# Conditioning products moved from GpSimd to TensorE in a fused 2+2-layer transformer kernel

## The chip, the cores and the metric

The kernel runs as one program on one core of one Trainium2 chip. The metric is the time of the program on the device in microseconds, as the median of several runs. Beside the runs there is one profiled execution, from which all rows come; it has a time of its own.

## The reference, cut to what matters

Two blocks of two layers follow one another on 256 tokens of width 1024, all in fp32. The second block is conditioned on one vector `c`: each of its two layers takes six rows of 1024 values (shift, scale and gate for the mixer and for the feed-forward part) from one product.

```python
x = first_block(x, mem, positions, ...)      # layer 0: pooled/latent attention; layer 1: gated recurrence
                                             # each: + cross attention to mem, + SwiGLU
cond = jax.nn.silu(c)                        # second block
for i in range(2):
    mod = cond @ ada_w[i] + ada_b[i]         # (1024) @ (1024, 6144): six rows
    sh_m, sc_m, g_m, sh_f, sc_f, g_f = split(mod, 6)
    h = rms_norm(x, norm_mix[i]) * (1 + sc_m) + sh_m
    y = dsa_attention(h) if i == 0 else s5_mixer(h)
    x = x + g_m * y
    h = rms_norm(x, norm_ffn[i]) * (1 + sc_f) + sh_f
    x = x + g_f * conv_ffn(h)
```

There are thus 12 rows of `mod`; each needs a 1024x1024 block of `ada_w`, which is 8 chunks of 128x1024 fp32 (512 KB), 96 chunks in all.

## The kernel before, in words

**Weights.** Nearly all products run on TensorE (PE) with each fp32 weight split in two fp32r parts. A chunk of 128x1024 is loaded by the queue of SyncE (SP) into a `raw` buffer; ScalarE (ACT) writes `hi` as a rounded copy (line 319); VectorE (DVE) writes `lo = raw - hi` (line 320; a few on POOL). PE then makes three products per operand pair (line 403, `mm`). Three `raw` and four `hi`/`lo` buffers exist, more in stages that open a ring (`ring`): `r1` (two more raw, three more split) holds from the first cross attention to the end of the first feed-forward part, `r4` (two more raw) in the sparse attention.

**Order.** `Builder` collects a list of steps in program order; each engine runs its own instructions in that order. Inside a stage the order is a string of two-letter codes: `EORD` (latent attention, `even`), `XORD` (cross attention, `xattn`), `OORD` (recurrence, `odd`), `DORD` (sparse attention, `dsa`). Work off to the side goes in two ways: a list `fill`, drawn by `gap`, and "lanes" (`side`), generators of which `add` puts a piece behind a step for every so many weight chunks that steps have used.

**Stages,** in us of the profile: latent attention 0 to 136, cross attention to 228, SwiGLU (`ffn(0)`) to 441, recurrence to 580, second cross attention to 650, second SwiGLU (`ffn(1)`) to 895, sparse attention (`dsa`) to 1070, convolutional feed-forward (`ffn(2)`) to 1293, state-space mixer to 1383, `ffn(3)` to the end. Between two stages `head` turns the normalised rows `h` by PE transposes (line 525, `norm_b`) into `xh`, `xl`.

**The conditioning rows** are made by `ada_gen` in a lane. SP loads a chunk into `fr` (line 733). POOL multiplies it by the column of silu(c) for its 128 inputs (line 752; line 750 for a row's first chunk) and adds it to `acc` (line 753). After eight chunks PE sums `acc` over the partitions with a 128x32 matrix of ones: four products, one for each 256 columns, each with its 32 output partitions (`w<-acc,ones`). DVE adds the bias (line 768), and a scale row is also multiplied by its norm's gain (line 770). Rows 0 to 7 are made from 50 us to the end of the recurrence, rows 10, 8, 9 in `ffn(2)`, row 11 in `ffn(3)`. `resid` and `mod_rows` use them later from DRAM.

**Attention values.** `pair_pv` multiplies the values of two heads by their probabilities. The values lie in `VP`, each head padded with 64 columns of zeros, so that the four products (two heads, two blocks of keys) all write 128 partitions of one bank. POOL fills `VP` with zeros first (lines 870, 1514).

**Second memory.** The cross attention of layer 1 has its own norm of `mem`. In `XORD` the steps `a0` to `a3` load it (from ACT's queue), take its squares (`na`), scale it (`na2`, line 683) and turn it (`nb`); `a2` and `a3` stand at the end.

**Tables.** `dsa_tables` and `odd_tables` (rotation tables and constants of the recurrence: some 50 DVE instructions on small tiles) are each one step of `ffn(0)`, behind its groups 6 and 12 of 22.

## Time and profile before

| | |
|---|---|
| median of 3 runs | 1596.26 us (1594.91 to 1597.49) |
| the profiled execution's own time | 1588.07 us |
| its span, first to last instruction | 1586.3 us |
| PE busy | 1437.9 us (91%) |
| DVE, ACT, POOL busy | 1227.6, 772.9, 719.5 us |
| mean granted clock of TensorE | 0.961 of full speed |
| chain that ended last | PE 37%, DVE 18%, ACT 6%, issue 4%, DMA 3%, POOL 1% of the span |
| read from memory | 302.45 MB, 198 GB/s over the span |

A busy share is an average over ten stages with different limits. Idle time of PE counts where the list of waits names what ended it. The granted clock stands at one of two levels, 2.4 GHz (1.0) and 1.2 GHz (0.5); in a window that mixes both, the mean stands between.

### The profile page before, as it was taken

Reading aid. Unit: us, or ns where it says so; the run is one execution under the profiler, and the core shown is the slowest. Engines: PE = TensorE matmul, PEld = TensorE weight load, DVE = VectorE, ACT = ScalarE, POOL = GpSimd, SP = SyncE. Lnnn points to the kernel's source line nnn. Section 1 sums busy time; section 2 is a strip of 40 time slices with the busy share of each in tenths; the row PEclk is TensorE's granted clock in tenths of the full one; section 3 lists DMA queues with packets and bytes.
Section 4 is the critical chain, followed back from the end, with each engine's and each line's share of the span. In section 5 each row is a group of like instructions: output and inputs, shape, how many; then the busy total and the mean of one; then the engine's idle time right before and its main releaser. Section 6 shows DMA issues by size and latency. Waiting matters only on the chain.

```text
span 1586.3 us, 25647 instructions
## 1 busy us (share of the span) xinstructions
PE 1437.9 (91%) x9852; PEld 1286.4 (81%) x9852; DVE 1227.6 (77%) x1734; ACT 772.9 (49%) x1286; POOL 719.5 (45%) x570
## 2 busy tenths in 40 slices
PE   8898989989998999899879698998999957899998
PEld 8787979978897879799778576678889845799997
DVE  5766577978957876877999779556887967689865
ACT  5654445334444765544434353656455543465542
POOL 4764567797965311412577522111864524105100
PEclk9999999999999999999989998999999979999999
DMA  6546758685754554665565444325887755667650
GB/s 239 201 175 236 257 178 275 233 319 215 282 184 152 161 184 148 211 220 168 208 202 169 161 137 142 107 67 187 299 281 279 266 123 178 221 229 255 220 177 27
DMA packets 90315, 316.24 MB, mean 199 GB/s; under 512 B 10464, under 2 KB 15504, under 8 KB 88912
## 3 DMA queue, kind: packets, MB, share of 16 engines
q1 hardware_dynamic: 77760, 277.57, 51.3%
q0 software_dynamic: 7216, 27.59, 5.3%
q10 hardware_dynamic: 5216, 9.44, 1.7%
q8 instruction: 77, 1.26, 0.3%
q14 instruction: 46, 0.38, 0.1%
HBM read 302.45 MB, written 11.06 MB: 198 GB/s over the span
## 4 chain that ended last, share of the span: by engine, by line
PE 37%; DVE 18%; ACT 6%; issue 4%; DMA 3%; POOL 1%; ACTq 0%; DVEq 0%; POOLq 0%
PE w L403 20%; PE a L403 13%; DVE lo L320 7%; ACT hi L319 2%; DMA raw<-in_down 2%; PE gl L403 1%; DVE sv L1935 1%; DVE cy L1267 1%; DMA raw<-in_up 1%; DMA U<-h 1%; DVE cy L1273 0%; DVE x L533 0%; PE w L525 0%; DVE h L480 0%; ACT e L813 0%
## 5 line engine op out<-in xcount | busy, mean ns | idle before, releaser
L320 DVE TENSOR_TENSOR lo<-raw,hi 128x1024 fp32r<-128x1024 f32 (+2 forms) x420 | 625.1, 1516 | 110.8 <-ACT hi L319 109.8
L319 ACT ACTIVATE hi<-raw 128x1024 fp32r<-128x1024 f32 (+2 forms) x430 | 437.5, 1047 | 111.0 <-DMA raw<-in_up 28.7
L403 PE MATMUL w<-xh,hi 128*128 128x256 f32 x1696 | 474.6, 285 | 16.0 <-DVE sg L1248 14.8
L403 PE MATMUL w<-xh,lo 128*128 128x256 f32 x1696 | 476.9, 285 | 10.3 <-DVE lo L320 9.7
L403 PE MATMUL w<-xl,hi 128*128 128x256 f32 x1696 | 466.4, 284 | 0.0
L403 PEld LDWEIGHTS w<-xh,hi 128*128 128x128 f32 x1696 | 322.5, 192 | 24.2 <-DVE sg L1248 15.7
L403 PEld LDWEIGHTS w<-xh,lo 128*128 128x128 f32 x1696 | 323.1, 192 | 14.2 <-DVE lo L320 14.2
L403 PEld LDWEIGHTS w<-xl,hi 128*128 128x128 f32 x1696 | 318.8, 191 | 3.1 <-ACT hi L319 0.2
L753 POOL TENSOR_TENSOR acc<-acc,fr 128x1024 f32<-128x1024 f32 x84 | 222.7, 2651 | 7.0
L752 POOL TENSOR_SCALAR fr<-fr,cs 128x1024 f32<-128x1024 f32 x84 | 168.4, 2005 | 126.2 <-DMA fr<-in_ada 125.5
L403 PE MATMUL a<-hi,gl 128*128 128x512 f32 x352 | 114.0, 398 | 7.2 <-DVE gl L397 7.2
L403 PE MATMUL a<-hi,gh 128*128 128x512 f32 x352 | 115.3, 401 | 4.0 <-ACT hi L319 3.2
L403 PE MATMUL a<-lo,gh 128*128 128x512 f32 x352 | 114.2, 398 | 0.6 <-DVE lo L320 0.5
L1267 DVE SCALAR_TENSOR_TENSOR cy<-w,cols,cy 128x254 f32<-128x254 f32 (+1 forms) x176 | 72.5, 473 | 23.9 <-ACT cy L1263 23.9
L403 PEld LDWEIGHTS a<-hi,gl 128*128 128x128 f32 x352 | 67.1, 191 | 23.0 <-DVE gl L397 7.8
L1247 ACT ACTIVATE sg<-w 128x256 f32<-128x256 f32 x44 | 16.8, 382 | 133.2 <-PE w L403 133.2
L403 PEld LDWEIGHTS a<-lo,gh 128*128 128x128 f32 x352 | 66.9, 190 | 17.2 <-DVE lo L320 2.0
L403 PEld LDWEIGHTS a<-hi,gh 128*128 128x128 f32 x352 | 61.7, 191 | 15.5 <-ACT hi L319 4.0
L396 ACT ACTIVATE gh<-cy 128x256 fp32r<-128x256 f32 x44 | 18.4, 418 | 95.0 <-DVE cy L1273 95.0
L500 POOL TENSOR_SCALAR sp<-ss 128x1 f32<-128x1 f32 x18 | 6.2, 345 | 121.9 <-ACT h L487 100.7
L750 POOL TENSOR_SCALAR acc<-fr,cs 128x1024 f32<-128x1024 f32 x12 | 16.5, 1376 | 93.0 <-DMA fr<-in_ada 51.1
L1263 ACT ACTIVATE cy<-w,cols 128x256 f32<-128x256 f32 x88 | 44.6, 557 | 28.2 <-PE w L403 27.8
(446 smaller groups left out, 2588.4 us busy)
## 6 DMA issues: line engine op xcount, KB each, us to landing
raw<-in_up SPq DMA_DIRECT2D x176, 512.0 KB, 4.4
fr<-in_ada SPq DMA_DIRECT2D x96, 512.0 KB, 5.2
raw<-in_down SPq DMA_DIRECT2D x88, 512.0 KB, 4.5
raw<-in_xa_k SPq DMA_DIRECT2D x16, 512.0 KB, 4.4
raw<-in_xa_v SPq DMA_DIRECT2D x16, 512.0 KB, 4.3
raw<-in_xa_q SPq DMA_DIRECT2D x16, 512.0 KB, 5.2
raw<-in_xa_o SPq DMA_DIRECT2D x16, 512.0 KB, 4.9
raw<-in_od_in SPq DMA_DIRECT2D x16, 512.0 KB, 3.3
```

Of the source, the lines that this page charges most:

```text
L319: nc.scalar.activation(hi[:, :n], t[:, :n], AF.Copy)
L320: (nc.gpsimd if j in self.lo_pool else nc.vector).tensor_sub(lo[:, :n], t[:, :n], hi[:, :n])
L396: nc.scalar.activation(hi, src, AF.Copy)
L403: self.nc.tensor.matmul(out, lhsT=a, rhs=b, start=start, stop=stop)
L500: g.tensor_scalar(p, ss[0], 1.0 / D, EPS, op0=OP.mult, op1=OP.add)
L750: g.tensor_scalar(acc, w, c, 0.0, op0=OP.mult, op1=OP.add)
L752: g.tensor_scalar(w, w, c, 0.0, op0=OP.mult, op1=OP.add)
L753: g.tensor_add(acc, acc, w)
L1247: nc.scalar.activation(sg, p[:, 0:S], AF.Silu)
L1263: nc.scalar.activation(y, u, AF.Identity, bias=cb[:, f:f + 1], scale=cw[:, 3 * f + 2:3 * f + 3])
L1267: nc.vector.scalar_tensor_tensor(y[:, s:], u[:, :S - s], cw[:, 3 * f + 2 - s:3 * f + 3 - s], y[:, s:], op0=OP.mult, op1=OP.add)
L1935: lambda e=e, out=out, p=p: e.tensor_mul(out, *p), lambda e=e, t=t, q=q: e.tensor_mul(t, *q),
```

## The change

**Products on PE.** `ada_gen` and its lanes go; so do the matrix of ones and all of POOL's multiplications and additions for the rows. Now `ada_mm(n)` takes n loaded chunks and makes four products for each on PE, with silu(c)'s column, repeated 32 times, as the stationary operand and 256 columns of the chunk as the moving one, all n accumulated in one bank. DVE then adds the bank to the row `modr`, which starts as the bias (line 777 of the changed kernel). SP loads the next chunks behind it. The places are written out: `i2` in the order strings is a pair of chunks, `ada=(2, 2, 0)` puts a pair ahead of each transposition of a head, and `ffn(2)` takes one chunk behind each of its groups 2 to 15. In all there are 41 pairs and 14 single chunks: 8 pairs in the latent attention, 4 in the cross attention, 2 in `ffn(0)`, 6 in the recurrence, 16 in `dsa`, 14 singles and a pair in and behind `ffn(2)`, 4 pairs in `ffn(3)`. Rows 5 to 8 are now made in `dsa`, where none was made, 10 and 9 in `ffn(2)`. The chunks have 4 buffers up to the recurrence, 3 in `dsa`, 2 after it.

**Values not padded.** `VP` holds the values alone, without zeros and without the fill. Each product of `pair_pv` has 64 stationary columns and writes its head's 64 partitions.

**Second memory.** `a0` to `a3` stand earlier and further apart in `XORD`; the load is issued by POOL.

**Tables.** `dsa_tables` and `odd_tables` become generators in a lane, a piece of one to three instructions for each chunk that `ffn(0)` uses.

**Smaller.** `r4` gives one more raw buffer in place of two. The order strings change elsewhere by the `i2` alone, and by `A0` ahead of `u3` in `EORD`.

```diff
-XORD = ('q0 q2 q4 f0 s0 s1 q6 p0 s2 p1 r0 a0 s3 w0 r1 p2 w1 r2 w2 p3 w3 a1 r3 w4 w5 a2 a3', 'q0 =0 q2 s0 q4 s1 p0 s2 q6 p1 r0 s3 r1 =1 p2 w0 w1 p3 w2 r2 w3 r3 w4 w5')
+XORD = ('q0 q2 q4 f0 s0 a0 s1 q6 p0 s2 i2 p1 r0 s3 a1 w0 r1 p2 i2 a2 w1 r2 w2 p3 i2 w3 r3 a3 w4 w5', 'q0 =0 q2 s0 q4 s1 p0 s2 q6 p1 r0 s3 r1 =1 p2 w0 w1 p3 w2 r2 w3 r3 w4 w5')
...
-OORD = 'x0 x1 g0 e0 x2 x3 f1 g1 e1 f1 R0 b0 g2 g3 l0 e2 s1 e3 f1 b1 f1 R1 s0 o0 f1 b2 f6 s2 b3 s3 d0 d1 o1 f1 f1 d2 d3 d4 d5'
...
+OORD = 'x0 x1 i2 g0 e0 x2 x3 f1 g1 e1 f1 i2 R0 b0 g2 g3 l0 e2 s1 e3 f1 i2 b1 f1 R1 s0 o0 f1 i2 b2 f6 s2 b3 s3 d0 d1 o1 f1 f1 d2 d3 d4 d5'
...
-    def head(self, fills=(0, 0, 0)):
+    def head(self, fills=(0, 0, 0), ada=(0, 0, 0)):
...
         for t in range(2):
             self.gap(fills[t])
+            self.ada_fill(ada[t])
             self.add((lambda t: lambda w: self.norm_b(t))(t))
         self.gap(fills[2])
+        self.ada_fill(ada[2])
...
-    def sincos(self, pool, ang, out_c, out_s, shape, tag):
+    def sincos_steps(self, pool, ang, out_c, out_s, shape, tag):
...
             nc.vector.tensor_scalar(n, ang, INV2PI, turn, op0=OP.mult, op1=OP.add)
+            yield
             nc.vector.tensor_scalar(n, n, MAGIC, None, op0=OP.add)
             nc.vector.tensor_scalar(n, n, -MAGIC, None, op0=OP.add)
             nc.vector.scalar_tensor_tensor(r, n, -PI_A, ang, op0=OP.mult, op1=OP.add)
+            yield
...
-    def ada_gen(self, rows, late=False):
-
-        nc, g = self.nc, self.nc.gpsimd
...
-            for k in range(8):
-                load()
-                w, c = tiles.pop(0), self.cs[:, k:k + 1]
-                if k == 0:
-                    g.tensor_scalar(acc, w, c, 0.0, op0=OP.mult, op1=OP.add)
-                else:
-                    g.tensor_scalar(w, w, c, 0.0, op0=OP.mult, op1=OP.add)
-                    g.tensor_add(acc, acc, w)
...
-            p = self.ps()
-            for j in range(4):
-                self.mm(p[32 * j:32 * j + 32, 0:256], self.ones, acc[:, 256 * j:256 * j + 256], True, True)
...
+            self.ada_rows = list(rows)
+            self.ada_todo = [8 * r + k for r in rows for k in range(8)]
...
+        self.steps.append((f, ()))
+
+    def ada_load(self):
+        while self.ada_todo and len(self.ada_tiles) < self.ada_bufs:
+            c = self.ada_todo.pop(0)
+            t = self.ada_pool.tile([P, D], F32, name="fr", tag="fr", bufs=self.ada_bufs)
+            self.nc.sync.dma_start(t, self.i["ada"][c])
+            self.ada_tiles.append((c, t))
...
+    def ada_store(self):
+        for r, m in self.ada_put:
+            self.nc.gpsimd.dma_start(self.mod[r].rearrange("(j n) -> j n", j=4),
+                                     m.rearrange("(j q) n -> j q n", q=32)[:, 0, :])
+            self.ada_rows.remove(r)
...
+    def ada_row(self, r):
+
+        new = lambda n: self.ada_pool.tile([P, 256], F32, name=n, tag=n, bufs=1)
+        m, ag = new("modr"), None
...
+    def ada_mm(self, n):
+
+        def f(w):
+            nc = self.nc
+            self.ada_store()
+            part, self.ada_tiles = self.ada_tiles[:n], self.ada_tiles[n:]
+            r = part[0][0] // 8
+            assert len(part) == n and part[-1][0] // 8 == r
+            if part[0][0] % 8 == 0:
+                self.ada_m = self.ada_row(r)
+            p = self.ps(name="ada")
+            for z, (c, t) in enumerate(part):
+                for j in range(4):
+                    self.mm(p[32 * j:32 * j + 32, 0:256], self.cs[:, c % 8:c % 8 + 1].to_broadcast([P, 32]),
+                            t[:, 256 * j:256 * j + 256], z == 0, z == n - 1)
+            m, ag = self.ada_m
             nc.vector.tensor_add(m, p[:, 0:256], m)
-            if ag is not None:
-                nc.vector.scalar_tensor_tensor(m, m, 1.0, ag, op0=OP.add, op1=OP.mult)
-            last = (r, m)
-        yield
-        store(*last)
-        if late:
-            self.close("frp")
+            if part[-1][0] % 8 == 7:
+                if ag is not None:
+                    nc.vector.scalar_tensor_tensor(m, m, 1.0, ag, op0=OP.add, op1=OP.mult)
+                self.ada_put.append((r, m))
+            self.ada_load()
+        return f
...
     def pair_pv(self, pts, vp, pair):
...
-        o = p[:, 0:S]
-        for a in range(2):
-            self.mm(o, vp(0, pair, a), pts[a][:, 0:S], a == 0, False)
-        for a in range(2):
-            self.mm(p[:, P:S], vp(1, pair, a), pts[a][:, S:3 * P], False, a == 1)
-        return o
+        for t, c, q in ((0, slice(0, S), slice(0, S)), (1, slice(P, S), slice(S, 3 * P))):
+            for a in range(2):
+                self.mm(p[64 * a:64 * a + 64, c], vp(t, pair, a), pts[a][:, q], t == 0, t == 1)
+        return p[:, 0:S]
...
+            st["VP"] = pl.tile([P, 2, 512], F32, name="VP")
             st["u"] = pl.tile([P, 4, S], F32, name="u")
...
-            self.xattn(0, fills=(1, 0, 1), mid=9, at2=[(lambda w: self.mem_load(1, self.nc.scalar), ()),
+            self.xattn(0, fills=(1, 0, 1), ada=(0, 2, 0), mid=9, at2=[(lambda w: self.mem_load(1, self.nc.gpsimd), ()),
                                                        (mem_a[0], ()), (mem_a[1], ()), late.pop(0)])
...
-            self.ffn(0, lambda: self.gain_row("od_norm"), self.act_swiglu(), fills=F0,
-                     at={6: [(lambda w: self.dsa_tables(), ())], 12: [(lambda w: self.odd_tables(), ())],
-                         **{j: [late.pop(0)] for j in A0}})
+            self.side("tab", 1.0, self.dsa_tables, self.odd_tables)
+            tab = self.lanes["tab"]
+            self.ffn(0, lambda: self.gain_row("od_norm"), self.act_swiglu(), fills=F0, ada=(2, 2, 0),
+                     at={8: [late.pop(0)], 19: [(self.pieces(tab, 1 << 30), ())]})
+            self.drain("tab")
...
-            self.ring("r4", 2, 0)
+            self.ring("r4", 1, 0)
+            self.ada_open("ad2", (5, 7, 6, 8), 3)
             self.dsa()
+            self.ada_close("ad2")
             self.unring("r4")
...
-            if LATE:
-                self.side("ada", RL, lambda: self.ada_gen(LATE, True))
+            self.ada_open("ad3", (10, 9), 2)
             self.ffn(2, lambda: (self.mod_gate(0, 1), self.mod_rows(1, 0)), self.act_conv(0), gate=True, nxt=self.to_u,
-                     fills=(2, 1, 1), last=LAST)
+                     fills=(2, 1, 1), last=LAST,
+                     at={j: [(self.ada_mm(1), ())] for j in range(2, 16)})
...
+            self.ada_fill(2)
+            self.ada_close("ad3")
...
-            self.side("ada", 0.25, lambda: self.ada_gen([11], True))
-            lane = self.lanes["ada"]
+            self.ada_open("ad4", (11,), 2)
             self.ffn(3, lambda: None, self.act_conv(1), gate=True, nxt=False, before=store,
-                     at={16: [(self.pieces(lane, 1 << 30), ()), (lambda w: self.mod_gate(1, 1), ())]})
+                     ada=(2, 2, 0), at={1: [(self.ada_mm(2), ())], 3: [(self.ada_mm(2), ())],
+                                        5: [(lambda w: (self.ada_store(), self.mod_gate(1, 1)), ())]})
+            self.ada_close("ad4")
```

PE at the head of the first cross attention; `h` is the normalised activation, `mh`/`ml` the memory. Before:

```order
L403 MATMUL w<-hi,mh 128x256
L403 MATMUL w<-lo,mh 128x256
L403 MATMUL w<-hi,ml 128x256
L525 MATMUL w<-cst,h 128x128 x16
L403 MATMUL w<-hi,mh 128x256
L403 MATMUL w<-lo,mh 128x256
L403 MATMUL w<-hi,ml 128x256
```

Now:

```order
L399 MATMUL w<-hi,mh 128x256
L399 MATMUL w<-lo,mh 128x256
L399 MATMUL w<-hi,ml 128x256
L521 MATMUL w<-cst,h 128x128 x8
L399 MATMUL ada<-fr,cs 32x256 x8
L521 MATMUL w<-cst,h 128x128 x8
L399 MATMUL w<-hi,mh 128x256
```

A pair of chunks, eight products, stands between the transposes of the two halves of the tokens.

DVE near the end of the same cross attention; `h<-mt` is the second memory's norm, `modr` a conditioning row, `ml<-w,mh` follows its transposition. Before:

```order
L320 TENSOR_TENSOR lo<-raw,hi 128x1024
L768 TENSOR_TENSOR modr<-w,modr 128x256
L770 SCALAR_TENSOR_TENSOR modr<-modr,ag 128x256
L397 TENSOR_TENSOR ol<-w,oh 128x512
L320 TENSOR_TENSOR lo<-raw,hi 128x1024
L1138 COPY pt<-w 128x512
L320 TENSOR_TENSOR lo<-raw,hi 128x1024
L397 TENSOR_TENSOR ol<-w,oh 128x512
L320 TENSOR_TENSOR lo<-raw,hi 128x1024 x2
L683 SCALAR_TENSOR_TENSOR h<-mt,rs,rowG 128x1024 x2
L397 TENSOR_TENSOR ml<-w,mh 128x4x128 x4
L320 TENSOR_TENSOR lo<-raw,hi 128x1024
```

Now:

```order
L1156 COPY pt<-w 128x512
L777 TENSOR_TENSOR modr<-ada,modr 128x256
L688 SCALAR_TENSOR_TENSOR h<-mt,rs,rowG 128x1024 x2
L316 TENSOR_TENSOR lo<-raw,hi 128x1024
L393 TENSOR_TENSOR ol<-w,oh 128x512
L316 TENSOR_TENSOR lo<-raw,hi 128x1024
L1156 COPY pt<-w 128x512
L777 TENSOR_TENSOR modr<-ada,modr 128x256
L316 TENSOR_TENSOR lo<-raw,hi 128x1024
L393 TENSOR_TENSOR ol<-w,oh 128x512
L393 TENSOR_TENSOR ml<-w,mh 128x4x128 x4
```

The scaling of `mt` stands three chunks (`lo<-raw,hi`) ahead of the rows that follow its transposition; before, the two were neighbours. There is an add to `modr` for every pair now.

PE in the softmax part of `dsa`; `kT,qT` are scores, `cst,e` transposes of the probabilities, `pt,VP` the values' products. Before:

```order
L403 MATMUL w<-pt,VP 128x256 x2
L403 MATMUL w<-pt,VP 128x128 x2
L824 MATMUL w<-cst,e 128x128 x6
L403 MATMUL w<-kT,qT 128x128
L403 MATMUL w<-kT,qT 128x256
L403 MATMUL w<-kT,qT 128x128
L403 MATMUL w<-kT,qT 128x256
L403 MATMUL w<-pt,VP 128x256 x2
L403 MATMUL w<-pt,VP 128x128 x2
```

Now:

```order
L399 MATMUL w<-kT,qT 128x256
L399 MATMUL w<-kT,qT 128x128
L399 MATMUL w<-kT,qT 128x256
L399 MATMUL ada<-fr,cs 32x256 x8
L399 MATMUL w<-pt,VP 64x256 x2
L399 MATMUL w<-pt,VP 64x128 x2
L845 MATMUL w<-cst,e 128x128 x6
L399 MATMUL w<-kT,qT 128x128
L399 MATMUL w<-kT,qT 128x256
L399 MATMUL w<-kT,qT 128x128
L399 MATMUL w<-kT,qT 128x256
```

The products with `VP` have 64 stationary columns in place of 128, and a pair of chunks stands next to each of the first groups.

## Rows read from the trace of the kernel before

**Rows 1.** Windows: stretch, length, busy us by engine (instructions), PEclk, DMA share, GB/s

```profile
228.00:441.00 213.00, 198.22 (x1421) 183.55 (x1421) 181.43 (x177) 90.28 (x128) 172.30 (x88) 0.97 0.72 255
895.00:1070.00 175.00, 158.51 (x795) 125.14 (x794) 124.25 (x296) 87.67 (x177) 45.02 (x63) 0.96 0.37 124
960.00:990.00 30.00, 25.14 (x96) 19.58 (x97) 28.97 (x67) 11.76 (x15) 6.14 (x4) 0.83 0.40 128
```

**Rows 2.** Waits of PE, whole span: waiting <- waited for, total us, times, longest

```profile
PE w L403 <- POOL acc L753: 15.2, 4, 7.0
PE w L2043 <- DMA U<-h: 11.5, 1, 11.5
PE w L525 <- DVE h L482: 6.0, 4, 3.5
PE w L525 <- DVE h L683: 4.9, 2, 4.0
```

**Rows 3.** Page, part 5, the products on POOL: busy us, mean ns | idle before

```profile
L753 POOL TENSOR_TENSOR acc<-acc,fr 128x1024 f32<-128x1024 f32 x84 | 222.7, 2651 | 7.0
L752 POOL TENSOR_SCALAR fr<-fr,cs 128x1024 f32<-128x1024 f32 x84 | 168.4, 2005 | 126.2 <-DMA fr<-in_ada 125.5
```

**Rows 4.** Groups by form, DVE, line 320: first 220 to 445 us, then 990 to 1072

```profile
L320 DVE TENSOR_TENSOR lo<-raw,hi 128x1024 fp32r<-128x1024 f32 x67 | 128.0, 1937 | 9.4 <-ACT hi L319 9.2
...
L320 DVE TENSOR_TENSOR lo<-raw,hi 128x1024 fp32r<-128x1024 f32 x15 | 18.4, 1239 | 10.0 <-ACT hi L319 10.0
```

**Rows 5.** Timeline of DVE, 205 to 224 us: start, length, instruction, idle before it

```profile
215.53 3.44 DVE L320 TENSOR_TENSOR lo<-raw,hi 128x1024 fp32r<-128x1024 f32 x1 [1.09 <-ACT hi L319]
219.70 1.28 DVE L683 SCALAR_TENSOR_TENSOR h<-mt,rs,rowG 128x1024 f32<-128x1024 f32 x1 [0.72 <-POOL rs L436]
```

**Rows 6.** Timeline of POOL, 212 to 222 us

```profile
215.52 2.38 POOL L753 TENSOR_TENSOR acc<-acc,fr 128x1024 f32<-128x1024 f32 x1
```

**Rows 7.** Windows: the seven stretches after a wait in which the clock is low, summed

```profile
350.10:353.10 3.00, 3.00 (x18) 2.19 (x19) 1.92 (x4) 0.00 (x0) 1.83 (x2) 0.51 0.92 351
sum 30.00, PE 27.91 PEld 24.09 DVE 21.38 ACT 11.11 POOL 17.74; mean PE 3.99 PEld 3.44 DVE 3.05 ACT 1.59 POOL 2.53
```

**Rows 8.** Timeline of PE, 124.9 to 127 us

```profile
124.64 0.40 PE L403 MATMUL a<-hi,ol 128*128 128x512 f32 x1
124.97 0.64 PE L403 MATMUL w<-acc,ones 128*32 128x256 f32 x8
125.53 1.58 PE L403 MATMUL w<-pt,VP 128*128 128x256 f32 x8
126.87 0.48 PE L403 MATMUL a<-hi,oh 128*128 128x512 f32 x1
```

**Rows 9.** Tile acc, PE: duration ns min/median/max

```profile
L403 PE MATMUL w<-acc,ones x96: 378/403/636, 125.0 to 1506.6; 128*32 128x256 f32 x96
```

**Rows 10.** Waits of PE in 56:66, 136:150, 376:380 and 470:484, in turn

```profile
PE w L403 <- DVE ol L397: 1.7, 1, 1.7
...
PE w L403 <- DVE xl L397: 6.1, 1, 6.1
...
PE w L403 <- DVE lo L320: 1.7, 1, 1.7
...
PE w L403 <- ACT xbh L396: 3.8, 1, 3.8
```

**Rows 11.** Timeline of DVE, 139 to 148.7 us

```profile
138.44 8.74 DVE L320 TENSOR_TENSOR lo<-raw,hi 128x1024 fp32r<-128x1024 f32 x5
```

**Rows 12.** Waits of PE in 1080 to 1296 us

```profile
PE w L403 <- DVE lo L320: 6.3, 8, 1.4
PE a L403 <- ACT hi L319: 3.2, 1, 3.2
```

**Rows 13.** Groups of DVE, the add of a finished row

```profile
L768 DVE TENSOR_TENSOR modr<-w,modr 128x256 f32<-128x256 f32 x12 | 5.0, 418 | 4.7 <-PE w L403 4.5
```

**Rows 14.** Tile fr: from issue to landing, all 96 loads

```profile
DMA to landing us min/median/max: 3.1/5.2/8.6
```

More of the change, by code (lines that the diff above doesn't have):

```diff
@@ L630, in setup @@
         self.cs = k.tile([P, 8], F32, name="cs")
-        self.ones = k.tile([P, 32], F32, name="ones")
         nc.vector.memset(self.mhalf, -0.5)
@@ L657, in sincos @@
             nc.vector.tensor_scalar(r, r, SAFE_PI, -SAFE_PI, op0=OP.min, op1=OP.max)
+            yield
             nc.scalar.activation(out, r, AF.Sin)
+    def sincos(self, *a):
+        for _ in self.sincos_steps(*a):
+            pass
     def mem_load(self, l, q):
@@ new lines, in ada_open @@
+    def ada_open(self, name, rows, bufs, pool=None):
+        def f(w):
+            self.ada_pool, self.ada_bufs = pool() if pool else self.open(name), bufs
+            self.ada_rows = list(rows)
+            self.ada_todo = [8 * r + k for r in rows for k in range(8)]
+            self.ada_tiles, self.ada_put = [], []
+            self.ada_load()
[6 more added lines that the diff above has]
+            self.ada_tiles.append((c, t))
@@ L777, in open, with ada_close, f, ada_fill @@
+    def ada_close(self, name):
+        def f(w):
+            self.ada_store()
+            assert not self.ada_rows and not self.ada_tiles, (self.ada_rows, len(self.ada_tiles))
+            if name:
+                self.close(name)
+        self.steps.append((f, ()))
+    def ada_fill(self, *ns):
+        for n in ns:
+            if n:
+                self.steps.append((self.ada_mm(n), ()))
     def open(self, name, bufs=1, side="left"):
@@ L946, in kvk @@
                 self.t1([p, p], w[0], c1, 2, 512, 512, True, True, toks=(t,))
-                pv = p.rearrange("p (g a n) -> p g a n", g=4, a=2)
-                for a in range(2):
-                    nc.vector.tensor_copy(st["VP"][:, t, :, a, a * 64:a * 64 + 64], pv[:, :, a, :])
+                nc.vector.tensor_copy(st["VP"][:, t, :], p)
             nc.scalar.activation(st["KT"][64:96, 1:8, :], self.bcast(st["KT"][64:96, 0, :], 1, 7), AF.Copy)
@@ L1074, in even @@
             elif c[0] == "A":
-                self.side("ada", RA[0], lambda: self.ada_gen([r for r in range(12) if r not in LATE + (11,)]))
+                self.ada_open(None, (1, 0, 2, 4, 3), 4, lambda: self.adap)
+            elif c[0] == "i":
+                self.ada_fill(k)
             elif c[0] == "f":
@@ L1164, in xattn @@
         o = f"xa_o{l}"
-        self.head(fills)
+        self.head(fills, ada)
         for c in XORD[l].split():
@@ L1175, in xattn @@
                 self.gap(mid)
+            elif c[0] == "i":
+                self.ada_fill(k)
             elif c[0] == "a":
@@ L1181, in xattn, with ffn @@
         add(lambda w: (self.close("xat"), self.end_o()))
-    def ffn(self, l, nxt_rows, act, gate=False, before=None, nxt=True, fills=(0, 0, 0), every=0, at=None, last=0):
+    def ffn(self, l, nxt_rows, act, gate=False, before=None, nxt=True, fills=(0, 0, 0), every=0, at=None, last=0,
+            ada=(0, 0, 0)):
         nc = self.nc
@@ L1223, in ffn @@
         add(begin)
-        self.head(fills)
+        self.head(fills, ada)
         for j in range(NF):
@@ L1430, in odd @@
         od = lambda n: (("od_in", n), ("od_in", n + 1))
-        self.head(fills)
+        self.head(fills, ada)
         step = {"g": gates, "e": gate_end, "R": lambda n: lambda w: roots(n)(w), "s": scan}
@@ L1473, in dsa_tables @@
         self.rB = self.keep.tile([P, 3, 2, 2, 32], F32, name="rB")
-        self.sincos(pl, ang, self.rA[:, 0, :, 0, :], self.rB[:, 0, :, 0, :], [P, 2, 32], "ds")
+        yield from self.sincos_steps(pl, ang, self.rA[:, 0, :, 0, :], self.rB[:, 0, :, 0, :], [P, 2, 32], "ds")
         g = pl.tile([P, 2, 2, 32], F32, name="dg")
@@ L1657, in f @@
                 for t in range(2):
-                    pv = z[t].rearrange("p (g a n) -> p g a n", g=4, a=2)
-                    for a in range(2):
-                        nc.scalar.activation(st["VP"][:, t, 4 * b:4 * b + 4, a, a * 64:a * 64 + 64], pv[:, :, a, :],
-                                             AF.Copy)
+                    nc.scalar.activation(st["VP"][:, t, 512 * b:512 * b + 512], z[t], AF.Copy)
             return f
@@ L2258, in f @@
             nc.gpsimd.tensor_copy(self.posf, self.pos)
-            nc.gpsimd.memset(self.ones, 1.0)
         self.add(f)
@@ L2325, in build @@
         if upto >= 3:
-            self.side("ada", RA[3])
-            self.odd(fills=(1, 0, 1))
+            self.odd(fills=(1, 0, 1), ada=(2, 2, 0))
             self.dump("dbg3")
-        self.drain("ada")
+        self.ada_close(None)
         if upto >= 4:
```

74 lines of the change are left out of this document (27 added, 47 removed).

## The prediction

> **What bounds the kernel now.** I read the stretches first [rows 1]. In `ffn(0)` PE is busy 198 of 213 us, so PE sets the pace there; but DVE, at 181 us, has little left. In 960 to 990, inside `dsa`, it is the other way: DVE is busy 28.97 of 30 us and PE waits. PE's list of waits comes next [rows 2]: in four places it stands for `acc`, 15.2 us in all, because POOL's chain of products [rows 3] is late.
>
> That chain does a second harm. A `lo` of 128x1024 takes 1239 ns late in `dsa`, where no row is made, and 1937 ns on average from 220 to 445 us [rows 4]. One case shows the mechanism: a `lo` begins at 215.53 us and takes 3.44 us [rows 5]; POOL's addition beside it begins at 215.52 and takes 2.38 [rows 6], and the rest, 1.07 us, is close to the time of a `lo` alone. So DVE stood still while POOL added. Behind it the second memory's norm, which waits for a small POOL operation queued behind the addition, comes late [rows 5], and PE waits 4.9 us for it [rows 2].
>
> The third view is the granted clock. After a long wait TensorE runs some microseconds at 1.2 GHz: 350.1 to 353.1 us shows 0.51, and seven such stretches hold 27.91 us of PE work [rows 7], which would have taken half of that. A wait costs more than its length.
>
> **The products on PE.** The nearest row is the sum with the ones: eight records (four products, two passes each) last 0.64 us from the first start to the last end [rows 8], and one lasts 0.403 [rows 9], so the second pass starts 0.24 us behind the first and the four products run side by side. Two passes are 0.48 us. The group starts 0.33 us after a product of 512 columns whose like follow each other in 0.23 us, and 0.56 us pass until the next instruction [rows 8]: 0.10 to enter and 0.08 to leave. A single chunk is thus 0.66 us, a pair 1.14. In all 96 x 0.48 + 55 x 0.18 = 56.0 us come, 12 x 0.66 = 7.9 us go: **+48.1 us** of PE work.
>
> The entry and exit are a change of the array's shape. The Trainium skill (TensorEngine Tiling (Array Packing), section Tiling Modes) says that changing the tiling mode drains the engine. By that rule alone, a change could cost the rest of a product's way through the array, 0.40 less 0.23 us [rows 8], or 0.17; two changes at 67 places would be 22.8 us in place of the 12.1 that I use, and the sum 10.7 us worse. The row is for the same change of shape, so I keep the row.
>
> **Values not padded.** A pair of heads takes 126.87 - 125.53 = 1.34 us on PE [rows 8]. With 64 columns each, the two heads can stand in the array together. No row shows 64 columns in two places; the four groups of 32 [rows 8, 9] are nearest, and they run at once. So 0.67 us and 0.18 for the change of shape: 12 x 0.49 = **-5.9 us**. The ends are +2.2 (no overlap, the shape's change alone) and -8.0. The zero fill on POOL and the fewer copies cost nothing either way: they lie ahead of their use, under projections.
>
> **Waits that go.** For `acc`, 15.2 us, and for the second memory's norm, 4.9 [rows 2]: POOL is free then, and the norm stands three chunks earlier. Waits behind a stretched `lo` are in the short stretches [rows 10]: 1.7 at 63 us, 1.7 at 377 (there the tables' burst on DVE helps to cause it, and it is cut in pieces), 3.8 at 479, and half of the 6.1 at 142, since five `lo` in that place take 8.74 us [rows 11] where 5 x 1.24 = 6.2 would do, and some overlap is lost. In `ffn(2)` it is 6.3 us for `lo` and 3.2 for a late chunk [rows 12], whose load was queued on SP behind loads that wait for POOL. That makes 19.7 us. With the seven slow stretches, 14.0 us [rows 7], **-53.8 us**. The ends: -25 if what is late next (DVE's own queue, in the recurrence above all) takes half of it; -60 if waits shorter than those listed go too.
>
> **What of the products is hidden.** Six pairs stand in the part of `dsa` where DVE is the limit [rows 1]: 6.8 us. The first pair of `dsa` stands before its norm is ready, 1.1; one pair lies behind `ffn(2)` where PE waits 11.5 us for U, 1.1; two at the head of `ffn(3)` lie in the 6.0 us for `h` [rows 2], 2.3; one in what is left at 142 us [rows 10], 1.1; in the recurrence and the softmax part of `dsa` I count 2.9. Together **-15.3 us**; ends 8 and 30. The other 40 us or so lie on a busy PE.
>
> **DVE's adds.** 43 more at 0.418 us [rows 13] make 18 us. Most lie under PE: in `ffn(0)` PE needs 198.22/22 = 9.0 us for a group and DVE, with the 47 us of stretching below taken off, (181.43 - 47)/22 = 6.1 [rows 1, 4]. On the path are the six where DVE is the limit: **+2.5 us**. Such an add waits on DVE until PE has come to its pair, with the next `lo` queued behind it; that costs nothing where PE holds split chunks for several microseconds. SP's loads of chunks wait for PE in the same way, with weight loads behind them; those are four or more chunks ahead. One raw buffer fewer in `dsa` costs nothing while DVE is the limit.
>
> **Sum:** 48.1 - 5.9 - 53.8 - 15.3 + 2.5 = -24.4 us. The profiled execution took 1588.07 us, so it would take 1563.7. It lies 8.2 us below the median of the runs shown, 1596.26; the same step from there gives **1572 us**.
>
> **Rivals.** *Chunks come late (slower).* PE takes its work in order, and a pair whose chunks have not landed stops it. A chunk lands 5.2 us after its issue, at most 8.6 [rows 14]. In `dsa` 16 pairs share 175 us [rows 1], 10.9 us each, and closer in the softmax part; with three buffers, one chunk of each pair is only requested when the pair before is done. If SP holds it back so that 15 pairs wait 2.5 us each, that is 37 us, and the time 1609. It decides from 24.4/15 = 1.6 us each. For it: SP issues in order. Against: 5.2 is half of 10.9. Chance 0.11.
>
> *The relief does not come (no change).* PE's waits are taken by the next late thing and the products fill what was won: if half of the 53.8 us returns, 1599; if 24 us, 1596. For it: DVE is nearly full in `ffn(0)` [rows 1]. Against: that fullness is itself stretched, 67 x (1937 - 1239) ns = 47 us of it [rows 4]. Chance 0.13.
>
> *More comes.* Waits go to the end of -60, 25 us of products are hidden, the pairs of heads give 8: 1572 - 6.2 - 9.7 - 2.1 = 1554. For it: nothing on POOL stretches DVE in the early stages any more. Chance 0.14.
>
> *The heads do not run side by side*, so that part does not do what it says: +8 us, 1580, inside the forecast.
>
> **How the numbers follow.** The forecast's own case (1560 to 1590) has 0.62. The range 1553 to 1597 leaves out the lower half of the third rival, the slower one, and part of the second, some 0.2. A measurement tells 0.2%, 3.2 us, from no change. Faster: 0.62, 0.14 and a third of the second rival, 0.80; same 0.07; slower 0.13.
>
> **What would show it.** Right: no wait of PE on POOL for a row, `lo` near 1.24 us in `ffn(0)`, no low clock at 350 and 437 us, a pair at about 1.1 us, `pt,VP` at about 0.85 us per pair of heads, PE some 42 us busier in nominal work. Wrong: waits of PE for `fr`, a longer `dsa` by more than 15 us, or `lo` still near 1.9 us, which would mean that it was not POOL that stretched it.

## The result and the profile after

The changed kernel takes 1607.11 us (median of 4 runs, 1605.45 to 1609.75) beside 1595.59 us for the kernel before on the same chip: ratio 1.0075, 95% interval 1.0053 to 1.0098. It is slower by 0.75%, where 1572 us and a gain were forecast, and it lies above the range.

The profiled execution has a span of 1608.0 us. I cut both traces at the end of each stage's last residual addition on DVE (`x<-x,a`); a stage's time runs from one such end to the next (the first from the span's start).

| stage | before | after | after, less before |
|---|---|---|---|
| latent attention (with the prologue) | 134.3 | 135.3 | +1.0 |
| first cross-attention | 98.3 | 89.9 | -8.4 |
| `ffn(0)` | 221.7 | 211.2 | -10.5 |
| recurrence | 136.4 | 139.3 | +2.9 |
| second cross-attention, `ffn(1)` | 299.1 | 303.1 | +4.0 |
| `dsa` | 180.4 | 216.0 | +35.6 |
| `ffn(2)` | 218.6 | 214.2 | -4.4 |
| state space and `ffn(3)` | 294.1 | 296.1 | +2.0 |

The last column adds up to 22.2 us, twice the difference of the medians: the profiled execution before is 7.5 us under its median and the one after 2.6 above, so a difference of two or three us in one stage says little. Everything but `dsa` is 13.4 us shorter together; `dsa` alone turns the sign. So the question is what happened in `dsa`, and whether `ffn(0)` gave all that it could.

Part of the relief is there at once. POOL is almost idle in `ffn(0)`, DVE has 113 us of work where it had 181 [rows 1], and a `lo` there is back at the time it had where POOL made no row [rows 4]. Windows of the changed kernel, in the same three stretches:

```profile
228.00:441.00 213.00, 205.25 (x1482) 192.13 (x1480) 112.79 (x179) 91.66 (x131) 6.24 (x15) 0.98 0.52 175
895.00:1070.00 175.00, 146.23 (x876) 105.61 (x874) 108.60 (x271) 70.28 (x131) 32.59 (x45) 0.92 0.54 191
960.00:990.00 30.00, 26.36 (x144) 19.12 (x143) 26.91 (x62) 10.55 (x13) 7.91 (x4) 0.94 0.52 192
```

Groups by form of DVE, 220 to 436 us, the changed kernel (busy us, mean ns | idle before):

```profile
L316 DVE TENSOR_TENSOR lo<-raw,hi 128x1024 fp32r<-128x1024 f32 x68 | 81.0, 1221 | 17.5 <-ACT hi L315 17.5
```

From 895 to 1070 us, which is most of `dsa`, the picture is the reverse: PE, DVE and ACT all have *less* to do per microsecond than before, and the clock is lower, 0.92. When all engines are idler, something outside them is likely to hold the chain. The groups of DVE and PE, and the DMA issues (KB each, median us to landing), name it:

```profile
L777 DVE TENSOR_TENSOR modr<-ada,modr 128x256 f32<-128x256 f32 x55 | 23.0, 418 | 55.9 <-DMA modr<-in_ada_b 52.9 <-PE ada L399 2.7 <-PE w L1675 0.3
L399 PE MATMUL ada<-fr,cs 128*32 128x256 f32 x768 | 57.1, 402 | 20.5 <-DMA fr<-in_ada 15.8 <-ACT Kt L1990 3.7 <-ACT pt L846 0.8
L755 POOL DMA_DIRECT2D modr<-in_ada_b x12 | 6.9, 575 | 28.9 <-DMA mod<-modr 28.8
```

```profile
modr<-in_ada_b POOLq DMA_DIRECT2D x12, 128.0 KB, 5.2
```

DVE stands 52.9 us for a transfer, at the add of a pair. In the kernel before, the same add (12 times, once a row) waited for PE alone [rows 13]. The transfer is the row's bias, which the add takes from `modr`. The head of `ffn(0)` shows the whole path: POOL, then DVE, then PE of the changed kernel (start, length, instruction, idle before it):

```profile
229.66 0.58 POOL L746 DMA_DIRECT2D mod<-modr  x1
235.09 0.57 POOL L755 DMA_DIRECT2D modr<-in_ada_b  x1 [4.85 <-DMA mod<-modr]
```

```profile
240.43 0.42 DVE L777 TENSOR_TENSOR modr<-ada,modr 128x256 f32<-128x256 f32 x1 [9.42 <-DMA modr<-in_ada_b]
240.77 1.28 DVE L393 TENSOR_TENSOR xl<-w,xh 128x512 fp32r<-128x512 f32 x2
```

```profile
230.07 1.07 PE L399 MATMUL ada<-fr,cs 128*32 128x256 f32 x16
231.07 1.09 PE L521 MATMUL w<-cst,h 128*128 128x128 f32 x8
232.09 1.07 PE L399 MATMUL ada<-fr,cs 128*32 128x256 f32 x16
240.91 1.97 PE L521 MATMUL w<-cst,h 128*128 128x128 f32 x8 [7.75 <-DVE modr L777]
```

There is one `modr`. POOL issues the store of the finished row at 229.66, waits 4.85 us for its landing, and only then asks for the next row's bias; that takes another 5 us. PE's product for the row was over at 231; the add comes at 240.43. PE stops for 7.75 us, and what releases it is the add itself: the four banks of `ps` serve in turn, the first pair's product still lies in the one that the next transposes need, and only the add frees it. Behind the add, in DVE's order, stand the `xl` of the transposes as well; at the head of `dsa` it is such an `xl` that PE waits for:

```profile
904.53 0.63 PE L399 MATMUL a<-hi,xl 128*128 128x320 f32 x1 [5.91 <-DVE xl L393]
```

Of the 10 us from 237 PE is busy 6.09, at the lower clock level:

```profile
237.00:247.00 10.00, 6.09 (x28) 5.86 (x29) 5.70 (x8) 3.08 (x4) 0.12 (x1) 0.50 0.49 178
```

In `dsa` DVE's waits for a bias are 10.27 us (902.55), 8.50 (1004.42) and 5.40 (1045.23), 24.2 of the 52.9 us. Of the nine waits, six (38.2 us) come behind a store; the other three stand at the first row of a list that `ada_open` opens, as at 902.55, with no store ahead.

The kernel before paid none of this. Its `ada_gen` asked for the bias at the fifth chunk of the row (`if k == 4`), and POOL was so slow that this was long before the add. A row around the start of `ffn(0)` in the kernel before, POOL's timeline and DVE's, has 35 us between the two:

```profile
226.03 0.64 POOL L757 DMA_DIRECT2D modr<-in_ada_b  x1
```

```profile
260.79 0.42 DVE L768 TENSOR_TENSOR modr<-w,modr 128x256 f32<-128x256 f32 x1
```

A second loss stands beside it: PE waits 15.8 us for chunks (`fr`), 13.2 of it in `dsa`. One of these waits, in SP's, PE's and DVE's timelines of the changed kernel:

```profile
940.77 10.17 SPq L307 DMA_DIRECT2D raw<-in_at_q  x2
950.99 0.90 SPq L741 DMA_DIRECT2D fr<-in_ada  x2
```

```profile
942.86 1.07 PE L399 MATMUL ada<-fr,cs 128*32 128x256 f32 x16
950.71 0.64 PE L399 MATMUL ada<-fr,cs 128*32 128x256 f32 x8
955.37 1.08 PE L399 MATMUL ada<-fr,cs 128*32 128x256 f32 x8 [4.03 <-DMA fr<-in_ada]
```

```profile
949.37 1.22 DVE L316 TENSOR_TENSOR lo<-raw,hi 128x1024 fp32r<-128x1024 f32 x1
```

SP issues a weight load at 940.77; the next gets out only at the end of that row, when DVE's `lo` of 949.37 has freed a raw buffer. PE was done with the pair before at 943.9, and its chunk buffers were free from then on; the requests that fill them stand in the same queue behind the weight load and follow at 950.99, some 7 us later, after PE has already begun the next pair.

### The profile page after: what moved, and what is told of

The parts are those of the page before. It is cut to its first block, busy times and chain, and to the rows that moved or that the text cites. A ratio compares the mean times of both kernels' runs of the same rounds, so it can differ in the third digit from the quotient of the medians.

```text
span 1608.0 us, 26876 instructions
## 1 busy us (share of the span) xinstructions
PE 1474.5 (92%) x10524; PEld 1288.6 (80%) x10524; DVE 1085.2 (67%) x1775; ACT 770.8 (48%) x1282; POOL 305.4 (19%) x389
## 4 chain that ended last, share of the span: by engine, by line
PE 64%; DVE 16%; DMA 7%; ACT 6%; issue 5%; POOL 2%; ACTq 0%; DVEq 0%; POOLq 0%; SPq 0%
PE w L399 36%; PE a L399 21%; DVE lo L316 5%; DMA modr<-in_ada_b 2%; ACT hi L315 2%; PE ada L399 2%; DVE sv L1963 1%; PE gl L399 1%; PE w L521 1%; ACT e L834 1%; DMA mod<-modr 1%; DVE x L529 1%; DMA raw<-in_up 1%; PE w L381 1%; DMA fr<-in_ada 1%
## 5 line engine op out<-in xcount | busy, mean ns | idle before, releaser
L316 DVE TENSOR_TENSOR lo<-raw,hi 128x1024 fp32r<-128x1024 f32 (+2 forms) x420 | 519.8, 1266 | 124.8 <-ACT hi L315 124.0
L399 PE MATMUL w<-xh,hi 128*128 128x256 f32 x1696 | 475.7, 286 | 19.5 <-DVE sg L1269 15.8
L399 PE MATMUL ada<-fr,cs 128*32 128x256 f32 x768 | 57.1, 402 | 20.5 <-DMA fr<-in_ada 15.8
L1269 DVE TENSOR_TENSOR sg<-sg,w 128x256 f32<-128x256 f32 x44 | 18.4, 418 | 82.3 <-ACT sg L1268 82.3
L777 DVE TENSOR_TENSOR modr<-ada,modr 128x256 f32<-128x256 f32 x55 | 23.0, 418 | 55.9 <-DMA modr<-in_ada_b 52.9
L399 PE MATMUL a<-hi,oh 128*128 128x512 f32 x160 | 56.0, 416 | 0.0
```

What stands on the lines that cost most here:

```text
L316: (nc.gpsimd if j in self.lo_pool else nc.vector).tensor_sub(lo[:, :n], t[:, :n], hi[:, :n])
L399: self.nc.tensor.matmul(out, lhsT=a, rhs=b, start=start, stop=stop)
L777: nc.vector.tensor_add(m, p[:, 0:256], m)
L1269: nc.vector.tensor_mul(sg, sg, p[:, S:2 * S])
```

## The experiments

Each ratio is against the kernel before, run on the same chip beside it. A difference of two of these runs carries the intervals of both, some 3 to 5 us.

| run | us | ratio (95% interval) | `dsa` | DVE waits for the bias | PE waits for chunks |
|---|---|---|---|---|---|
| the change | 1607.11 | 1.0075 (1.0053 to 1.0098) | 216.0 | 52.9 | 15.8 |
| `bias_two` | 1581.76 | 0.9925 (0.9902 to 0.9947) | 203.5 | 6.7 | 18.7 |
| `chunk_queue` | 1609.49 | 1.0096 (1.0064 to 1.0128) | 215.1 | 53.3 | 15.9 |
| `both` | 1579.58 | 0.9922 (0.9893 to 0.9951) | 203.7 | 0.8 | 15.6 |
| `early` | 1570.81 | 0.9847 (0.9825 to 0.9870) | 190.4 | 0.9 | 3.5 |
| `two_late` | 1599.68 | 1.0031 (1.0010 to 1.0052) | 212.8 | 22.1 | 19.6 |
| `chunks_only` | 1599.48 | 1.0030 (1.0011 to 1.0050) | 210.3 | 44.2 | 2.7 |
| `no_rows` | 1573.61 | 0.9874 (0.9830 to 0.9919) | 181.4 | 30.5 | 3.3 |
| `no_rows_raw` | 1575.19 | 0.9868 (0.9843 to 0.9893) | 181.3 | 27.0 | 4.7 |
| `no_ada` | 1528.36 | 0.9581 (0.9555 to 0.9608) | 178.7 | | |
| `unpadded` | 1591.13 | 0.9972 (0.9955 to 0.9988) | 178.8 | | |

### The bias loaded ahead

The gain `ag` had a buffer of its own that stands empty for most rows. So two buffers serve in turn, with no memory added: a row's bias goes into the one that the row before does not use, and it is asked for at that row's second pair (behind a row with a gain: at its end).

```diff
...
+    def ada_tile(self, n, side):
+        return self.ada_pool.tile([P, 256], F32, name=n, tag=("modr", "ag")[side], bufs=1)
+
+    def ada_bias(self):
+        if self.ada_turn:
+            self.ada_next = self.ada_tile("modr", self.ada_side)
+            self.ada_side = 1 - self.ada_side
+            self.nc.gpsimd.dma_start(self.ada_next, self.i["ada_b"][self.ada_turn.pop(0)])
...
             if part[0][0] % 8 == 0:
-                self.ada_m = self.ada_row(r)
+                self.ada_m = self.ada_next, None
+            elif part[0][0] % 8 == n:
+                if r % 3 == 1:
+                    self.ada_m = self.ada_m[0], self.ada_tile("ag", self.ada_side)
+                    nc.gpsimd.dma_start(self.ada_m[1], self.i["ada_g"][r // 3])
+                else:
+                    self.ada_bias()
...
                 if ag is not None:
                     nc.vector.scalar_tensor_tensor(m, m, 1.0, ag, op0=OP.add, op1=OP.mult)
+                    self.ada_bias()
```

> The bias of the next row is loaded into the other of the two row buffers a pair or more ahead, so that the first add of a row no longer waits on DVE for the store of the row before and for the load behind it; nothing else differs. Row-start theory (DVE stands 52.9 us in 9 such waits in the changed kernel, 24.2 us of it in the sparse attention where DVE is the limit, and 7.75 us of PE at the head of the first feed-forward): the DMA wait of the adds falls under 5 us, the sparse attention from 216.0 us to 190 to 198, the whole to 1577 to 1587 us, faster than the kernel before. Late-chunk theory (PE waits 13.2 us for chunks in the sparse attention): the DVE wait goes as well, but the attention stays over 208 us and the whole over 1598. Full-PE theory (the attention is longer because 32 chunks of product stand on PE there): likewise no gain, 1600 to 1609.

Measured: 1581.76 us, 25 us less than the change, and faster than the kernel before. `dsa` fell by 12.5 us and `ffn(0)` by 10.2, to 201.0. The groups of DVE and PE in this run:

```profile
L784 DVE TENSOR_TENSOR modr<-ada,modr 128x256 f32<-128x256 f32 x55 | 22.9, 417 | 11.0 <-DMA modr<-in_ada_b 6.7 <-PE ada L399 4.2
L399 PE MATMUL ada<-fr,cs 128*32 128x256 f32 x768 | 56.0, 396 | 19.7 <-DMA fr<-in_ada 18.7 <-ACT pt L854 0.8
```

And `ffn(0)` of this run, in a window of 202 us: PE busy throughout, at full clock, DVE with 90 us to spare.

```profile
228.00:430.00 202.00, 201.75 (x1474) 188.69 (x1474) 112.00 (x177) 91.59 (x131) 6.85 (x13) 1.00 0.54 184
```

The row-start theory holds for the whole and in place: 46 us of DVE's waits went, and 25 us of time, so somewhat over half of the wait was on the path. Two of its figures were missed: the wait that is left is 6.7 us and not under 5, and `dsa` ended longer (203.5 against 190 to 198), with PE's wait for chunks still there.

### The chunks from another queue

```diff
+            self.ada_q = self.nc.scalar if name == "ad2" else self.nc.sync
...
-            self.nc.sync.dma_start(t, self.i["ada"][c])
+            self.ada_q.dma_start(t, self.i["ada"][c])
```

> In the sparse attention alone the chunks of the table are asked for from ScalarE's queue and not behind the weights on SP's queue; the row buffers stay as in the changed kernel. Late-chunk theory: PE's 13.2 us of waits for chunks fall under 4 us and the attention from 216.0 us to about 200, the whole to 1590 to 1597. Row-start theory: PE's waits for chunks fall, but DVE is the limit there and the whole gains 0 to 6 us (1601 to 1608). Full-PE theory: no gain.

Measured: 1609.49 us, no gain. It did not do what it was made for: PE still waits 15.9 us for chunks, now mostly in one piece, 10.85 us, at the first pair of `dsa`. So it tells nothing about the theories.

### Both

> Both edits together, the bias loaded ahead into the other row buffer and the sparse attention's chunks from ScalarE's queue. If the two waits are what was lost and lie in different places, their gains add: attention 175 to 185 us, whole 1565 to 1578. If the row-start wait is all, it equals the first of the two runs within 3 us. If PE itself is full there, 1600 or more.

Measured: 1579.58 us, the same as the first run within 2.2 us. By the letter of the expectation this speaks for the row start alone; but the waits for chunks were not removed, so it can't tell. Here too the waits for chunks, gone from the middle of `dsa`, stand at its head, as ACT's timeline and PE's show:

```profile
875.82 11.17 ACTq L744 DMA_DIRECT2D fr<-in_ada  x5
887.04 0.86 ACT L315 ACTIVATE hi<-raw 128x792 fp32r<-128x792 f32 x1 [11.40 <-DMA fr<-in_ada]
```

```profile
882.00 1.08 PE L399 MATMUL ada<-fr,cs 128*32 128x256 f32 x8 [10.02 <-DMA fr<-in_ada]
885.51 1.08 PE L399 MATMUL ada<-fr,cs 128*32 128x256 f32 x8 [2.44 <-DMA fr<-in_ada]
```

ACT comes to the first requests only at 875.82, behind the norm of this stage, and is then itself held by the later ones, which need a chunk buffer that PE has yet to free.

### The first chunks early, the first pairs later

The next kernel keeps both edits, asks for the first three chunks from SP's queue, where they are issued sooner, and lets the first two pairs of `dsa` stand later, behind `a0 b0` and behind `k0`.

```diff
-DORD = "i2 a0 b0 i2 k0 k1 T0 ...
+DORD = "a0 b0 i2 k0 i2 k1 T0 ...
...
+            self.ada_q = self.nc.sync
             self.ada_todo = [8 * r + k for r in rows for k in range(8)]
             self.ada_tiles, self.ada_put = [], []
             self.ada_load()
+            self.ada_q = self.nc.scalar if name == "ad2" else self.nc.sync
```

> The two edits together, with two more: the first three chunks of the sparse attention are asked for from SP's queue (later ones from ScalarE's), and its first two pairs stand one step later each, behind the two first projections and behind the first key step. In the run of both edits PE stood 10.0 and 2.4 us for chunks at the head of the attention and nowhere else in it. If these waits were what hid the gain of the queue's move, the attention falls from 203.7 us to 192 to 196 and the whole to 1568 to 1574. If PE's other work in the attention only moves up to the next late thing, 1577 to 1583.

Measured: 1570.81 us, ratio 0.9847, the best version here; `dsa` 190.4 us. Both waits are all but gone, in the groups of DVE and PE:

```profile
L786 DVE TENSOR_TENSOR modr<-ada,modr 128x256 f32<-128x256 f32 x55 | 22.9, 416 | 4.7 <-PE ada L399 3.8 <-DMA modr<-in_ada_b 0.9
L399 PE MATMUL ada<-fr,cs 128*32 128x256 f32 x768 | 54.2, 392 | 4.3 <-DMA fr<-in_ada 3.5 <-ACT pt L856 0.8
```

All work of the change is in this kernel: the same 768 records of products, the same 55 adds, the unpadded values. What differs is when and from where transfers are asked for, and the place of two pairs; that takes 36 us off. What the earlier requests and the later pairs each give was not measured apart.

### Store or load: which half of the round trip

> As the run with the bias loaded ahead, with the two row buffers taken in turn, but the bias is asked for where the changed kernel asks for it, at the row's first pair. The load then waits for no store, and only its own way (from the issue to the landing) is left in front of the first add. If the store's landing, in front of the load, is what made the wait long (8 of the 9 longest waits of the changed kernel hold both), DVE's wait for the bias falls from 52.9 us to 15 to 25 and the whole lands between, 1588 to 1597. If asking late is the cost, whatever the buffer, the wait stays over 35 us and the whole at 1600 or more. If the store is all, as with the load ahead: under 10 us and 1579 to 1585.

The edit is that of `bias_two` with `ada_bias()` called at the row's first pair. Measured: DVE's wait for the bias 22.1 us, as the first theory said, but the time only 1599.68, above the 1588 to 1597 that went with it and next to the 1600 of the second theory. Half of what is left lies in one wait, the longest of all, in DVE's list of waits (total, times, longest) and in POOL's and DVE's timelines:

```profile
DVE modr L781 <- DMA modr<-in_ada_b: 22.1, 8, 10.9
```

```profile
884.59 0.65 POOL L436 DMA_DIRECT2D rowG<-mod  x1
885.49 0.54 POOL L436 DMA_DIRECT2D rowA<-mod  x1 [0.25 <-DVE h L476]
886.45 0.53 POOL L436 DMA_DIRECT2D rowB<-mod  x1 [0.42 <-DVE Kt L1995]
886.98 0.54 POOL L759 DMA_DIRECT2D modr<-in_ada_b  x1
```

```profile
897.12 0.42 DVE L781 TENSOR_TENSOR modr<-ada,modr 128x256 f32<-128x256 f32 x1 [10.92 <-DMA modr<-in_ada_b]
```

This is the first row of `dsa`: no row was stored ahead of it, but the bias is issued behind three rows that are spread over all partitions, and it takes 10 us to come; that these rows are the reason was not tested. The expectation's aside, that 8 of the 9 longest waits of the changed kernel hold a store's landing too, is wrong: it is 6 of 9, and the longest, at 902.55, is not among them. The second buffer alone takes off 7 us (1607.1 to 1599.7); asking early takes off another 18 (to 1581.8). Asking late is the larger half.

### The chunks alone

> As the run called early (chunks of the sparse attention from ScalarE's queue but the first three, its first two pairs one step later), with the changed kernel's single row buffer and its late load of the bias. If the two losses add, it keeps 11 us of the 36 between the changed kernel and early: 1594 to 1598, the attention 203 to 206. If the chunks' waits are hidden behind DVE's row-start waits, 1603 to 1608 and the attention still over 210.

Measured: 1599.48 us, `dsa` 210.3. PE's wait for chunks falls to 2.7 us, DVE's for the bias stays at 44.2. The groups:

```profile
L779 DVE TENSOR_TENSOR modr<-ada,modr 128x256 f32<-128x256 f32 x55 | 23.0, 418 | 51.2 <-DMA modr<-in_ada_b 44.2 <-PE a L399 4.5 <-PE ada L399 2.4
L399 PE MATMUL ada<-fr,cs 128*32 128x256 f32 x768 | 55.0, 396 | 3.5 <-DMA fr<-in_ada 2.7
```

The time lies between the two expectations, the stage at the edge of the second. The bias alone gives 25.3 us, the chunks alone 7.6, both 36.3: the two losses add within the intervals.

### What the rows cost in `dsa`, and the raw buffer

```diff
-            self.ada_open("ad2", (5, 7, 6, 8), 3)
+            self.steps.append((lambda w: [self.nc.gpsimd.dma_start(self.mod[r], self.i["rows"][0]) for r in (5, 6, 7, 8)], ()))
...
-        for c in DORD.split():
+        for c in DORD.replace("i2 ", "").split():
```

> The sixteen pairs of the sparse attention (rows 5 to 8 of the modulation) are left out: their products, adds, chunk loads, bias loads and stores; other values stand in these rows instead, so the output is not the reference's. It prices all that the four rows cost where they stand. Their products alone are 32 chunks at 0.59 us, 19 us. Full-PE theory: the attention falls from 216.0 us by about 19 to 22, to 194 to 197. Row-start and late-chunk theories: it falls by 40 to 50, to 166 to 176, under the 180.4 of the kernel before.

Measured: 1573.61 us, `dsa` 181.4: the four rows cost 34.6 us there in the change, 22.1 in `bias_two`, and 9.0 in `early` (190.4 less 181.4). The full-PE theory (19 to 22) falls for the change as it stands. The 40 to 50 us of the other two theories are 5 us or more too much; the stage does not fall below its 180.4 us of the kernel before. The whole does not come under `early` either: the waits for the bias in the other stages are still in it (30.5 us).

With `self.ring("r4", 2, 0)` in place of `("r4", 1, 0)` on top of that:

> The run without the sparse attention's four rows, with the second raw buffer for weights there that the change took away. The forecast put that buffer at nothing: within 2 us of the 1573.6 of the run without the rows. If the weights' loads were held up by its lack, 3 to 8 us faster, the attention 174 to 179 instead of 181.4.

Measured: 1575.19 us, `dsa` 181.3. Without the rows, the lack of the raw buffer shows no cost. With the rows in place it was not tested, and there the request for chunks stood behind a weight load that waited for just such a buffer (940.77), so a part of the chunks' wait could be its price.

### The relief and the heads by themselves

`no_ada` leaves out all 96 chunks: `ada_mm` returns an empty step, and the twelve rows are filled from another tensor as above.

> The changed kernel with all 96 chunks left out: no products, adds, chunk loads, bias loads or row stores anywhere; other values stand in the twelve rows, so the output is not the reference's. It prices the relief alone, apart from what the products cost. The forecast's relief: 53.8 us of waits, 5.9 of heads and 7.9 of sums with the ones gone from the kernel before, so 1526 to 1532. If the relief came only by half, 1552 to 1560. The price of the 96 chunks on PE is then the distance to the run with the bias loaded ahead (1581.8): 43 by the forecast (56.0 of products, 15.3 hidden, 2.5 of adds).

Measured: 1528.36 us, inside the forecast's window. The relief is 66.6 us (1594.97 less 1528.36) where the forecast's terms make 67.6. It is an upper measure: the loads of the chunks are left out as well. The price of the chunks, to the run that the expectation named, is 1581.76 less 1528.36, 53.4 us where 43 was forecast; only to `early`, with most of the waits for chunks gone, is it 42.4.

`unpadded` is the kernel before with the parts of the change on `VP` and `pair_pv` alone.

> The kernel before, with the values not padded as the only edit (the two heads of a pair side by side on PE, no zero fill, fewer copies). The forecast's term: -5.9 us in twelve pairs of heads, 8 of them in the sparse attention and 4 in the latent one, ends +2.2 and -8.0, so 1588 where the kernel before takes 1594. Rival: PE waits for the softmax in both places, the shorter products only wait longer: within 2 us of the kernel before.

Measured: ratio 0.9972 (0.9955 to 0.9988), a gain of 2 to 7 us. The two heads do run side by side: 96 products of the same mean length keep PE busy for 11.3 us in place of 19.3 (first the kernel before, then this run). What of the gain is theirs, and what comes from the fill and the copies that go with the zeros, no run tells.

```profile
L403 PE MATMUL w<-pt,VP 128*128 128x256 f32 (+1 forms) x96 | 19.3, 347 | 0.9 <-ACT pt L825 0.9
L403 PE MATMUL w<-pt,VP 128*64 128x256 f32 (+1 forms) x96 | 11.3, 352 | 0.9 <-ACT pt L825 0.9
```

## Why the prediction was wrong

**The step that failed** is the one on DVE's adds: "Such an add waits on DVE until PE has come to its pair, with the next `lo` queued behind it; that costs nothing where PE holds split chunks for several microseconds." It priced the add's wait on PE, which is indeed small (2.7 us in all), and forgot the add's *other* operand. The sum has no term for the transfer that brings the bias. It was in the two kernels: the load moved from the row's fifth chunk, behind which POOL still had three chunks of work, to its first pair, into a single `modr` that POOL has just begun to store. The row on which I leaned [rows 13] shows an add that waits for PE alone *because* the load came early, and the change took that away. The missing term is 25.3 us of the 35 by which the forecast was off; the rest is about what the chunks cost.

**The rival on chunks** named a real mechanism with the wrong size: 15 waits of 2.5 us were assumed, and PE waits 13.2 us in 5 in `dsa`. Removing them is worth 7.6 us alone and 11.0 on top of the bias (1581.76 to 1570.81). The text saw that with three buffers one chunk of a pair is asked for late; it compared a landing of 5.2 us with 10.9 us between pairs, and put no size on the time for which the request itself stands in SP's queue, some 7 us in the case at 943.9.

**The other terms held together.** `early`, which differs from the change in the asking and in the place of two pairs, takes 1570.81 us where 1572 was forecast. The four runs of `no_ada` lie between 1524.71 and 1533.39, so that relief and price each agree within 1 us is finer than the runs can tell.

| term | forecast | measured |
|---|---|---|
| relief (waits, heads, sums with the ones) | 67.6 | 66.6 (kernel before, less `no_ada`) |
| price of the 96 chunks (56.0 + 2.5 - 15.3) | 43.2 | 42.4 (`early` less `no_ada`); 53.4 with the waits for chunks |
| heads alone | 5.9 (-2.2 to 8.0) | 1.9 to 7.2 |
| a `lo` in `ffn(0)` | near 1.24 us | 1.22 |
| raw buffer in `dsa` | 0 | no gain without the rows (1.6 us longer); not tested with them |

That the price agrees is in part luck. A pair was put at 1.14 us and a single chunk at 0.66, with 0.10 us to enter and 0.08 to leave, read up to the start of the next instruction [rows 8]. But the product behind that one starts late as well. PE's timeline of the changed kernel around a pair and around a single chunk:

```profile
964.53 0.40 PE L399 MATMUL a<-hi,xl 128*128 128x512 f32 x1
964.86 1.07 PE L399 MATMUL ada<-fr,cs 128*32 128x256 f32 x16
965.86 0.50 PE L399 MATMUL a<-hi,xh 128*128 128x512 f32 x1
966.20 0.40 PE L399 MATMUL a<-lo,xh 128*128 128x512 f32 x1
```

```profile
1126.32 0.63 PE L399 MATMUL a<-hi,gl 128*128 128x512 f32 x2
1126.87 0.64 PE L399 MATMUL ada<-fr,cs 128*32 128x256 f32 x8
1127.44 0.38 PE L399 MATMUL w<-xh,hi 128*128 128x256 f32 x1
1127.66 0.28 PE L399 MATMUL w<-xl,hi 128*128 128x256 f32 x1
```

From 964.53 to 966.20 are 1.67 us, where two steps of 0.23 would do: the pair costs 1.20 us (1.15 where products of 128 columns follow). From 1126.32 to 1127.66 are 1.34 us, where two steps of 0.23 and one of 0.12 would do: the chunk costs 0.76. For 41 pairs and 14 singles that makes, as an estimate from these, 58 to 60 us, 2 to 4 more than the 56.0 forecast. So as much more is hidden than I counted, or other terms make up for it; no run tells these apart.

By the Trainium skill (TensorEngine Tiling (Array Packing), section Tiling Modes), a change of the tiling mode drains the engine; the forecast worked that out to as much as 0.34 us for the two changes around a step. A pair less a single chunk gives 0.44 us for a chunk, and so 0.32 for entry and exit together. The trace comes close to that estimate; the 0.18 that the sum used was too low, and its 0.48 for a chunk too high.

**Of what would show it wrong**, two came true: waits of PE for `fr`, and a `dsa` longer by over 15 us. Neither pointed at the main cause, since I had not thought of DVE waiting for a transfer.

**What stays open.** The recurrence, where a wait of 3.8 us for `xbh` was to go, got 2.9 us longer (139.8 us in `early` as well). In `no_ada` it takes 133.4, so the relief there is 3.0 us and its six pairs with their adds put 5.9 on; where they wait was not looked into. The second cross-attention and `ffn(1)`, which hold no pair, are 4 us longer together in the profiled run. Half of that can be the execution: `unpadded`, with the code of the kernel before in these stages, takes 301.7 us there beside 299.1. No run was made for the rest.

## What to carry to other kernels

When work moves from a slow engine to a fast one, list every operand of its steps, not only the large ones: a transfer that was early because the old engine was slow becomes late without a line of it being "slower". An add that waits for a small load on an in-order engine costs what stands behind it there. And count a request's time from the moment when its buffer is free, with the time that it stands in its queue, and not from the issue to the landing alone; give it a second buffer *and* ask ahead, since the buffer alone took off 7 us of 25.
